# A hybrid retention and HGRN2 step on one core: level scores on column tiles, merged and moved short products, two-stream sums, and later starts of the first HGRN2 threads

## The chip, the cores and the metric

The kernel runs on one core of a Trainium2 chip, as one program. The metric is the device time of one execution in microseconds (us). Before the change it was 2616.91 us, the median of 3 runs (2615.58 to 2618.65). The engines of the core are named as in the profile: PE (TensorE, with PEld for its weight loads), DVE (VectorE), ACT (ScalarE), POOL (GpSimd) and SP (which issues most DMAs).

## The reference

One layer of a decoder for 272 prompt columns (16 meta tokens and 256 prompt tokens) and 8 sample columns, together 280, with a model width of 2048. A first half-step FFN (SwiGLU, width 5504) and a norm; a mixer; a norm; a second half-step FFN and a norm. The mixer projects `x @ w_in` to ten parts of 2048 and runs two recurrences:

```
def hgrn2_chunk(S, q, k, v, logf):
    b = jnp.cumsum(logf, axis=2)
    decay = exp(where(causal, b[i] - b[j], -inf))            # per feature d
    A = jnp.einsum('bhid,bhjd,bhijd->bhij', q, k, decay)
    o = einsum('bhij,bhjv->bhiv', A, v) + einsum('bhid,bhdv->bhiv', q * exp(b), S)
    S_new = exp(b_last) * S + einsum('bhjd,bhjv->bhdv', k * exp(b_last - b), v)
def retention_chunk(S, q, k, v):
    inner = einsum('bhid,bhjd->bhij', q, k) * D              # D: fixed decay per head
    o = einsum('bhij,bhjv->bhiv', inner, v) + einsum('bhid,bhdv->bhiv', q_dec, S)
    S_new = exp(lg * C) * S + einsum('bhjd,bhjv->bhdv', k_dec, v)
```

HGRN2 has 16 heads of 128, retention 8 heads of 256. The outputs are normed per head, gated, merged and projected by `w_out`. Prompt states and sample states are outputs too.

## The kernel before, in words

Features lie on the 128 partitions, tokens in the columns. A float32 weight block is streamed as 128x1024 raw values (`raw`, 512 KB a DMA, L184), cast on ACT to `whi` (L187), and its rest subtracted on DVE to `wlo` (L188); each such load serves 8 blocks of 128x128. `dense` (L203 to L219) does three matmuls a block: high by high, low by high, high by low, all of type float32r, with 264 or 280 columns. They are written as `Halves`: the columns lie in two halves and are read alternately, as two streams.

Phases in order: FFN 1 (L452), the projections with the mixer (L604 to L1075), the output projection, FFN 2, the last norm.

**The mixer's threads.** For each u from 0 to 7 there is a group of projections (`f, q_h, i_h, q_r, k_r, v_r`, each two column blocks of 128) and, one u later, the gates. After each of the 16 steps k of a projection, `dense` calls `pump` (L592), which counts down every open thread and, when a thread's count has run out, runs it to its next `yield n`; n is the number of pumps until it goes on. A thread is `mix_hg(u, ...)` (L713, two HGRN2 heads) or `mix_ret(u, ...)` (L945, one retention head). PE executes in the order in which this code writes its instructions (`manual_schedule`, L137): a thread's matmuls stand between two steps of a projection, and PE runs nothing past one that waits. The order on DVE, ACT and SP is set by a scheduler when the program is built; each engine then also works in that order. A thread is started by `start(gen, wait)` when its last projection is evacuated: `mix_hg` 3 pumps after `i_h`, but 30 for u = 1 (L642).

u = 0 is special: its first two groups of projections start before the first norm is finished. `Norm.first` and `Norm.second` (L365, L383) compute them on unnormed columns and correct the result on DVE (`corrected`, L388), while `normalise` (L402) writes the normed columns `xh` on ACT and `xl` on DVE (L407). For u = 0 the results `y` of `corrected` lie in row tiles, and for `i_h` ACT copies them to `v` (L639).

**mix_hg.** It makes Q, K and products on DVE and ACT (L716 to L744); then, for each of the two heads h, four transposes of `v` to a PSUM bank `pt` (L751: two of 128 columns, the 16 meta columns and the last 16), an ACT copy to `vth` (L752), an ACT copy of the last 16 to `vsm` (L753), a DMA of 8 of these rows to DRAM (L754) and the high and low parts `vm` of the first 16 (L755). `yield 1` stands after each head. Nine pumps later come sums over the features with a matrix of ones (`sums`, L227): `pd`, 512 columns, and per level `pl`. The causal score matrix `acc` is built in levels s = 1, 2, 4, 8, 16, 32, 64: in each, the second half of every pair of blocks of s tokens looks at the first half.

- s = 1 and 2: sums with ones (L782, L784), then DVE copies under a mask (L852).
- s = 4 and 8: one product of K (128 columns) with 192 columns for each head and half (L771).
- s = 16: four products of 128 key columns with 64 query columns each (L799), then one masked DVE copy (L852).
- s = 32: eight products of 32 by 32 on column tiles 0 and 64 of PE (`tile_position=(0, j)`, L794), then ACT copies.
- s = 64: four products of 64 by 64, all on the column tile at 0 (L789), then one ACT copy (L847).

Later steps: transposes of K (L868), states (L887, L889), the sample product `pq` on four column tiles (L901), an ACT copy `osh` of it (L905) and, 4 pumps later, the outputs (L912, L913, L709) and norms, with pauses of `8 + calm`.

**mix_ret.** Transposes of v and k (L965, L974), three score products in `psc` (L991; the third has 16 keys and 16 queries), the prompt state `psr` (L1008, seven float32r matmuls of 256 columns a half), the sample state `smr` scaled on ACT (L1025) and updated on DVE (L1028), the sample product `pqr` (L1039, two halves of 256 columns that DVE adds at L1044), then outputs (L1053) and the norm.

Plain float32 products appear in the records as two matmuls each, float32r products and transposes as one.

Of the kernel before, what the change touches and what calls it, by code (L numbers as in the profile page):

```python
# [14 lines left out]
ALU = mybir.AluOpType  # L15
# [3 lines left out]
P = 128  # L19
# [26 lines left out]
MASKED = 5  # L46

MASKS = {1: [0], 2: [1, MASKED], 4: [2], 8: [3, MASKED + 1], 16: [4]}
# [79 lines left out]
def trunk(ctx: ExitStack, tc: tile.TileContext, A, O):  # L128
# [98 lines left out]
    def sums(out, hilo, part=slice(None)):  # L227

        for i, x in enumerate(hilo):
            if isinstance(x, Halves):  # L230
                o, x = pairs(out), x[:]
            else:
                o, x = out, x[:, part]
            nc.tensor.matmul(o, ones_r, x, start=i == 0, stop=i == 1)
# [33 lines left out]
    class Norm:  # L268
# [114 lines left out]
        def second(self, block, outs, x0s):  # L383
            dense(block, KC, outs, xh, xl, [slice(x0, self.n + 2) for x0 in x0s])
            self.normalise()
            return self.corrected(outs, x0s)

        def corrected(self, outs, x0s):  # L388
            ys = []
            for i, (o, x0) in enumerate(zip(outs, x0s)):  # L390
                w = self.n - x0
                wgb = rp.tile([P, 2], F32, tag=f"wgb{i}", name="wgb")
                nc.scalar.copy(wgb, o[:, w : w + 2])
                y = self.row(("ls1", "ls2", "lnq", "rt")[i])[:, :w]
                nc.vector.scalar_tensor_tensor(
                    out=y, in0=self.mean[:, x0:], scalar=wgb[:, 0:1], in1=o[:, :w], op0=ALU.mult, op1=ALU.subtract)
# [134 lines left out]
    with tc.tile_pool(name="yp", bufs=1) as yp:  # L531
# [7 lines left out]
        with tc.tile_pool(name="mp", bufs=1) as mp:  # L539
# [37 lines left out]
            vsm = tmp("vsm", (P, 2, P))  # L577
# [26 lines left out]
            def project(groups):  # L604
                for grp in groups:

                    bank = mx_bank if grp[0] == (QKV_ORDER[2], 0) else acc_bank
                    outs = [bank(f"pj_{n}{c}") for n, c in grp]
                    x0s = [NMETA if n in LIVE else 0 for n, _ in grp]
                    if grp[0] == (QKV_ORDER[0], 0):  # L610
                        outs = norm1.first(block, outs, x0s)
                    elif grp[0] == (QKV_ORDER[2], 0):
                        outs = norm1.second(block, outs, x0s)
                    else:
                        dense(block, KC, outs, xh, xl, [slice(x0, T) for x0 in x0s], pump)
                    for j in range(0, len(grp), 2):
                        w = T - x0s[j]
                        evacuate(grp[j][0], grp[j][1], grp[j + 1][1], outs[j][:, :w], outs[j + 1][:, :w])

            def evacuate(n, c0, c1, o0, o1):  # L620
# [16 lines left out]
                elif n == "i_h":  # L637
                    v = tmp("v", (P, 2, T))
                    nc.scalar.copy(v[:, 0, :], o0)  # L639
                    nc.scalar.copy(v[:, 1, :], o1)  # L640

                    start(mix_hg(c0 // 2, st["f"], st["k"], st["q"], v), 30 if c0 == 2 else 3)  # L642
# [70 lines left out]
            def mix_hg(u, f, k, q, v):  # L713
# [31 lines left out]
                vt = tmp("vth", (P, 2, 2, P))  # L745
                vrow = []
                for h in range(2):

                    pt = mx_bank("pt")
                    for b, (t0, n) in enumerate(((NMETA, P), (NMETA + P, P), (0, NMETA), (T - NMETA, NMETA))):  # L750
                        nc.tensor.transpose(pt[:n, b * P : (b + 1) * P], v[:, h, t0 : t0 + n], ident)  # L751
                    nc.scalar.copy(vt[:, h], pt[:, : 2 * P].rearrange("p (b f) -> p b f", b=2))  # L752
# [6 lines left out]
                sums(pd.rearrange("p (i c) -> p i c", i=2), hilo, slice(0, 2))  # L759
                nc.vector.tensor_tensor(  # L760
                    out=acc.rearrange("p (b c) -> p b c", b=4), in0=pd.rearrange("p (b c) -> p b c", b=4),
                    in1=ident.unsqueeze(1).to_broadcast([P, 4, P]), op=ALU.mult)
                Tt = f
                for s in LEVELS:
# [18 lines left out]
                    elif s == 2:  # L783
                        sums(pl.rearrange("p (i c) -> p i c", i=2), hilo)  # L784
                    for h in range(2 if s > 8 else 0):
                        for b in range(2):
                            k0, q0, o = NMETA + b * P, b * P, (2 * h + b) * min(s, 64)
                            if s == 64:
                                nc.tensor.matmul(  # L789
                                    pl[0:s, o : o + s], K[:, h, k0 : k0 + s], Q[:, h, q0 + s : q0 + 2 * s],  # L790
                                    start=True, stop=True)
                            elif s == 32:
                                for j in (0, 64):
# [51 lines left out]
                    elif s >= 32:  # L845
# [4 lines left out]
                    else:  # L850
                        for j, mi in enumerate(MASKS[s]):
# [3 lines left out]
                                pl[:, j * SEQ : (j + 1) * SEQ].rearrange("p (n s) -> p n s", s=s))  # L855
# [72 lines left out]

                hilo = outputs(0)
# [15 lines left out]
            def mix_ret(u, q, k, v):  # L945
# [43 lines left out]
                for b, (col, l0, n, nk) in enumerate(SCORES):  # L989
                    for c in range(2):  # L990
                        nc.tensor.matmul(  # L991
                            psc[:nk, col : col + n], k[:, c, b * P : b * P + nk], q[:, c, l0 : l0 + n],
                            start=c == 0, stop=c == 1)
# [3 lines left out]
                mul(scr2[:NB2], psc[:NB2, c2:NSC], dt[:NB2, c2:])  # L997
                upper_upper_lower(sc2, scr2[:NB2])
# [3 lines left out]
                for c in range(2):  # L1002
                    pst = mx_bank("psr")
                    f = slice(c * P, (c + 1) * P)
                    pairs = [(ks[:, i, b, f], vs[:, j, b, :]) for b in range(2) for i, j in ((0, 0), (0, 1), (1, 0))]
                    pairs.append((ks2[:, c, :], vs2.rearrange("p c f -> p (c f)")))
                    for i, (kk, vv) in enumerate(pairs):
                        nc.tensor.matmul(pst[:, :256], kk, vv, start=i == 0, stop=i == 6)  # L1008
                    so = tmp("sro", (P, 256))
                    nc.scalar.copy(so, pst[:, :256])  # L1010
# [193 lines left out]
```

## Time and profile before

| what | value |
|---|---|
| median of 3 runs | 2616.91 us |
| the profiled execution | 2617.9 us |
| its span in the trace | 2616.1 us (1.8 us less) |
| mean granted TensorE clock | 0.998 |
| DVE busy | 1738.8 us (66%) |
| ACT busy | 1358.7 us (52%) |
| DMA | 536.26 MB, mean 205 GB/s |

The profile shows one execution. Its page gives busy time by engine, the span in 40 slices, the chain of work that ended last, and the costliest groups of instructions. The trace behind it answers finer questions: waits (who waited for whom), a timeline of single instructions in a window, and busy time and granted clock by window. Times in the timeline are in us from the span's start. A row of the timeline has the start, the time until its last instruction's end, engine, line, operation, what is written from what, shape, and how many instructions the row merges; in brackets the idle time before it and what ended that. Matmuls overlap: the distance between the starts of two rows tells what a matmul costs PE, not the time from its start to its end. Times before 770 us belong to FFN 1, from 740 to 1770 to the mixer, after that to the output projection and FFN 2.

### The profile page before, as it was taken

The page shows a single profiled execution, that of the slowest core. Times are in us where ns is not written, and L with a number is a line of the kernel's source. Part 1 is how long each engine was busy: PE and PEld are TensorE (multiplying, and loading weights), DVE is VectorE, ACT ScalarE, POOL GpSimd, SP SyncE. Part 2 cuts the span into 40 slices and gives each one's busy share as a digit, 9 for nine tenths or more (in the row PEclk, how much of TensorE's full clock was granted, in tenths as well). Part 3 has the DMA queues.
Part 4 walks back from the last instruction along what each step waited for, and adds up shares of the span by engine and source line. Part 5 has one row for each costly group of instructions (what it writes and reads, how often), then busy time and mean ns, then how long its engine had stood idle before and what let it go on. Part 6 is the DMA issues. An engine that isn't in the chain of part 4 may idle for free.

```text
span 2616.1 us, 54489 instructions
## 1 busy us (share of the span) xinstructions
PE 2593.6 (99%) x22576; PEld 2563.8 (98%) x22576; DVE 1738.8 (66%) x2961; ACT 1358.7 (52%) x2124; POOL 3.3 (0%) x38
## 2 busy tenths in 40 slices
PE   9999999999998999999999999999999999999999
PEld 9999999999998999999999999999999999999998
DVE  6445444565579788777878787876995555556555
ACT  5444444444465567656566656565564444444444
POOL 0000000000000000000000000000000000000000
PEclk9999999999999999999999999999999999999999
DMA  7555555565566786767676767666656666666664
GB/s 245 184 185 185 186 186 185 179 186 185 185 197 196 236 266 204 240 207 256 215 241 212 251 213 246 218 228 193 193 184 203 194 196 197 195 195 194 196 197 148
DMA packets 154584, 536.26 MB, mean 205 GB/s; under 512 B 17696, under 2 KB 25696, under 8 KB 154336
## 3 DMA queue, kind: packets, MB, share of 16 engines
q1 hardware_dynamic: 154048, 532.50, 63.5%
q8 instruction: 176, 2.88, 0.4%
q14 instruction: 72, 0.59, 0.1%
q10 hardware_dynamic: 288, 0.29, 0.0%
HBM read 502.12 MB, written 30.61 MB: 204 GB/s over the span
## 4 chain that ended last, share of the span: by engine, by line
PE 91%; DVE 5%; DMA 2%; ACT 1%; issue 1%; SPq 0%; DVEq 0%; ACTq 0%
PE up L217 35%; PE dn L217 18%; PE pj_k_r L217 3%; PE wo L217 3%; PE pj_q_h L217 3%; PE pj_v_r L217 3%; PE pj_g_r L217 3%; PE pj_f L217 3%; PE pj_q_r L217 3%; PE pj_g_h L217 3%; PE pj_a_r L217 3%; PE pj_a_h L217 3%; PE pj_i_h L217 3%; DVE wlo L188 2%; DMA smr<-in_sr 1%
## 5 line engine op out<-in xcount | busy, mean ns | idle before, releaser
L188 DVE TENSOR_TENSOR wlo<-raw,whi 128x1024 fp32r<-128x1024 f32 (+1 forms) x869 | 1061.8, 1223 | 718.5 <-ACT whi L187 711.0
L187 ACT CAST whi<-raw 128x1024 fp32r<-128x1024 f32 (+1 forms) x870 | 905.1, 1042 | 912.6 <-PE up L217 409.5
L217 PE MATMUL up<-xh,wlo 128*128 128x280 f32 (+1 forms) x2624 | 725.9, 280 | 0.4 <-DVE wlo L188 0.2
L217 PE MATMUL up<-xh,whi 128*128 128x280 f32 (+1 forms) x2624 | 725.6, 280 | 0.4 <-ACT whi L187 0.4
L217 PE MATMUL up<-xl,whi 128*128 128x280 f32 (+1 forms) x2624 | 725.4, 279 | 0.0
L217 PEld LDWEIGHTS up<-xh,wlo 128*128 128x128 f32 x2624 | 492.6, 189 | 1.2 <-DVE wlo L188 1.2
L217 PEld LDWEIGHTS up<-xh,whi 128*128 128x128 f32 x2624 | 492.6, 189 | 0.6 <-ACT whi L187 0.6
L217 PEld LDWEIGHTS up<-xl,whi 128*128 128x128 f32 x2624 | 492.6, 189 | 0.0
L217 PE MATMUL dn<-hh,whi 128*128 128x280 f32 (+1 forms) x1376 | 384.7, 280 | 0.0
L217 PE MATMUL dn<-hh,wlo 128*128 128x280 f32 (+1 forms) x1376 | 384.3, 279 | 0.0
L217 PE MATMUL dn<-hl,whi 128*128 128x280 f32 (+1 forms) x1376 | 384.3, 279 | 0.0
L217 PEld LDWEIGHTS dn<-hh,whi 128*128 128x128 f32 x1376 | 260.1, 189 | 0.1
L217 PEld LDWEIGHTS dn<-hl,whi 128*128 128x128 f32 x1376 | 260.1, 189 | 0.1
L217 PEld LDWEIGHTS dn<-hh,wlo 128*128 128x128 f32 x1376 | 260.1, 189 | 0.0
L217 PE MATMUL pj_g_r<-xh,whi 128*128 128x264 f32 x256 | 76.9, 300 | 0.0
L217 PE MATMUL pj_g_h<-xh,whi 128*128 128x264 f32 x256 | 73.5, 287 | 0.1
L217 PE MATMUL pj_v_r<-xh,whi 128*128 128x280 f32 x256 | 73.6, 288 | 0.0
L217 PE MATMUL pj_k_r<-xh,whi 128*128 128x280 f32 x256 | 73.5, 287 | 0.0
L217 PE MATMUL pj_g_h<-xh,wlo 128*128 128x264 f32 x256 | 71.1, 278 | 2.0 <-DVE wlo L188 2.0
L217 PE MATMUL pj_k_r<-xh,wlo 128*128 128x280 f32 x256 | 72.8, 284 | 0.1
L217 PE MATMUL pj_k_r<-xl,whi 128*128 128x280 f32 x256 | 72.7, 284 | 0.0
L217 PE MATMUL pj_v_r<-xl,whi 128*128 128x280 f32 x256 | 72.3, 283 | 0.0
(402 smaller groups left out, 5285.2 us busy)
## 6 DMA issues: line engine op xcount, KB each, us to landing
raw<-in_w_up SPq DMA_DIRECT2D x343, 512.0 KB, 4.2
raw<-in_w_in SPq DMA_DIRECT2D x320, 512.0 KB, 3.7
raw<-in_w_dn SPq DMA_DIRECT2D x172, 512.0 KB, 3.5
smr<-in_sr SPq DMA_DIRECT2D x32, 512.0 KB, 4.3
out_srs<-smr SPq DMA_DIRECT2D x32, 512.0 KB, 5.5
raw<-in_w_out SPq DMA_DIRECT2D x32, 512.0 KB, 3.4
smh<-in_sg SPq DMA_DIRECT2D x16, 512.0 KB, 4.8
vbr<-vrd SPq DMA_DIRECT2D x16, 512.0 KB, 4.3
```

The costliest lines, as they stand in the source:

```text
L187: nc.scalar.copy(hi[:, j:jn, :], raw[:, j:jn, :])
L188: nc.vector.tensor_tensor(out=lo[:, j0:j1, :], in0=raw[:, j0:j1, :], in1=hi[:, j0:j1, :].bitcast(F32), op=ALU.subtract)
L217: nc.tensor.matmul(o, w, t, start=start, stop=stop)
```

## The change

1. `sums` reads a pair of products as two streams: columns of the two products alternate, in `pd` and in `pl` of level 2. DVE reads the results with a step of two, and `pd` is multiplied by the identity in two DVE instructions for one.
2. `Norm.second` can write its result to a given place: for u = 0, `i_h` goes straight to `v`, without the ACT copies.
3. The thread of u = 0 starts 20 pumps after `i_h` (3 before), that of u = 1 46 pumps after (30 before). For u = 0 the pauses in the outputs are 8 (10 before).
4. In `mix_hg` the short transposes go: DVE copies the first and the last 16 columns of both heads to a tile `ends` (two copies), and one transpose of `ends` (64 columns) follows the two long transposes of head 1 and the ACT copy `vth` of head 1, in the same bank `pt`. `vsm`, the row DMAs and `vm` of both heads come after it.
5. Level 16: sixteen products of 16 by 16, on the column tiles 0, 32, 64 and 96; ACT copies in place of the masked DVE copy (and one mask less). Level 64: its two halves b on the column tiles 0 and 64; two ACT copies for one.
6. In `mix_ret` the third score product moves from `psc` to the bank of `pqr`, just ahead of the sample product, and so do the steps that follow it (`scr2`, `sc2`); the two halves of `pqr` are accumulated in PSUM, without DVE's add.
7. The prompt state `psr` reads `vs` as two streams; ACT copies the result with a step of two.

The diff, cut to its core:

```diff
@@ sums
+            elif len(x.shape) == 3 and x[:, part].shape[1] == 2:
+                o, x = pairs(out), x[:, part].rearrange("p a b -> p b a")
@@ Norm.corrected
-                nc.vector.tensor_scalar(out=y, in0=y, scalar1=-1.0, scalar2=wgb[:, 1:2], op0=ALU.mult, op1=ALU.add)
-                ys.append(y)
+                to = into[i] if i < len(into) else y
+                nc.vector.tensor_scalar(out=to, in0=y, scalar1=-1.0, scalar2=wgb[:, 1:2], op0=ALU.mult, op1=ALU.add)
+                ys.append(to)
@@ project, evacuate
-                        outs = norm1.second(block, outs, x0s)
+                        v = st["i_h"] = tmp("v", (P, 2, T))
+                        outs = norm1.second(block, outs, x0s, (v[:, 0, :], v[:, 1, :]))
-                    start(mix_hg(c0 // 2, st["f"], st["k"], st["q"], v), 30 if c0 == 2 else 3)
+                    start(mix_hg(c0 // 2, st["f"], st["k"], st["q"], v), {0: 20, 2: 46}.get(c0, 3))
@@ mix_hg
                 vt = tmp("vth", (P, 2, 2, P))
+                ends = tmp("ends", (P, 2, 2, NMETA))
+                nc.vector.tensor_copy(ends[:, :, 0, :], v[:, :, :NMETA])
+                nc.vector.tensor_copy(ends[:, :, 1, :], v[:, :, T - NMETA :])
                 for h in range(2):
                     pt = mx_bank("pt")
-                    for b, (t0, n) in enumerate(((NMETA, P), (NMETA + P, P), (0, NMETA), (T - NMETA, NMETA))):
-                        nc.tensor.transpose(pt[:n, b * P : (b + 1) * P], v[:, h, t0 : t0 + n], ident)
+                    for b in range(2):
+                        nc.tensor.transpose(pt[:, b * P : (b + 1) * P], v[:, h, NMETA + b * P : NMETA + (b + 1) * P], ident)
                     nc.scalar.copy(vt[:, h], pt[:, : 2 * P].rearrange("p (b f) -> p b f", b=2))
-                    nc.scalar.copy(vsm[:NMETA, h, :], pt[:NMETA, 3 * P :])
-                    vrow.append(rows_out(vsm[8:16, h, :], P, f"vh{h}"))
-                    upper_lower_upper(vm[:, h, :], pt[:NMETA, 2 * P : 3 * P])
+                    if h:
+                        x = pt[:64, 2 * P : 3 * P]
+                        nc.tensor.transpose(x, ends.rearrange("p c a t -> p (c a t)"), ident)
+                        nc.scalar.copy(vsm[:64], x)
+                        for c in range(2):
+                            vrow.append(rows_out(vsm[32 * c + 24 : 32 * c + 32, :], P, f"vh{c}"))
+                            upper_lower_upper(vm[:, c, :], x[32 * c : 32 * c + NMETA])
                     yield 1
@@ levels 16, 32, 64
                             if s == 64:
+                                j = 64 * b
                                 nc.tensor.matmul(
-                                    pl[0:s, o : o + s], K[:, h, k0 : k0 + s], Q[:, h, q0 + s : q0 + 2 * s],
-                                    start=True, stop=True)
-                            elif s == 32:
-                                for j in (0, 64):
+                                    pl[j : j + s, h * s : (h + 1) * s], K[:, h, k0 : k0 + s], Q[:, h, q0 + s : q0 + 2 * s],
+                                    start=True, stop=True, tile_position=(0, j))
+                            else:
+                                for j in range(0, P, 2 * s):
                                     nc.tensor.matmul(
                                         pl[j : j + s, o : o + s], K[:, h, k0 + j : k0 + j + s],
                                         Q[:, h, q0 + j + s : q0 + j + 2 * s], start=True, stop=True, tile_position=(0, j))
-                            else:
-                                o = (2 * h + b) * 64
-                                nc.tensor.matmul(
-                                    pl[:, o : o + 64], K[:, h, k0 : k0 + P],
-                                    Q[:, h, q0 : q0 + P].rearrange("p (n t s) -> p n t s", t=2, s=s)[:, :, 1, :],
-                                    start=True, stop=True)
+                calm = calm if u else 0
@@ mix_ret
-                for b, (col, l0, n, nk) in enumerate(SCORES):
+                for b in range(2):
+                    scores(psc[:, SCORES[b][0] :], b)
-                mul(scr2[:NB2], psc[:NB2, c2:NSC], dt[:NB2, c2:])
-                upper_upper_lower(sc2, scr2[:NB2])
-                        nc.tensor.matmul(pst[:, :256], kk, vv, start=i == 0, stop=i == 6)
+                        nc.tensor.matmul(pairs(pst[:, :256]), kk, vv.rearrange("p c f -> p f c"), start=i == 0, stop=i == 6)
-                    nc.scalar.copy(so, pst[:, :256])
+                    nc.scalar.copy(so.rearrange("p (c f) -> p c f", c=2), apart(pst[:, :256]))
                 pq = mx_bank("pqr")
+                scores(pq[:, 256:], 2)
-                                pq[32 * j : 32 * j + 32, 256 * e : 256 * e + 256], qdr[:, c, 32 * b : 32 * b + 32],
-                                sms[2 * e + c][:, j, :], start=c == 0, stop=c == 1, tile_position=(0, 32 * j))
+                                pq[32 * j : 32 * j + 32, :256], qdr[:, c, 32 * b : 32 * b + 32],
+                                sms[2 * e + c][:, j, :], start=e + c == 0, stop=e + c == 2, tile_position=(0, 32 * j))
+                mul(scr2[:NB2], pq[:NB2, 256 : 256 + NMETA], dt[:NB2, c2:])
+                upper_upper_lower(sc2, scr2[:NB2])
-                add(os, os, pq[:, 256:])
```

`scores(out, b)` is a new local function with the two accumulating products of one block b of `SCORES`, as L992 has them.

More of the change, by code (lines that the diff above doesn't have):

```diff
@@ L45 @@
 LEVELS = (1, 2, 4, 8, 16, 32, 64)
-MASKED = 5
-MASKS = {1: [0], 2: [1, MASKED], 4: [2], 8: [3, MASKED + 1], 16: [4]}
+MASKED = 4
+MASKS = {1: [0], 2: [1, MASKED], 4: [2], 8: [3, MASKED + 1]}
 W_LEVEL = 6
@@ L381, in first, with second, corrected @@
             return ys
-        def second(self, block, outs, x0s):
+        def second(self, block, outs, x0s, into=()):
             dense(block, KC, outs, xh, xl, [slice(x0, self.n + 2) for x0 in x0s])
             self.normalise()
-            return self.corrected(outs, x0s)
-        def corrected(self, outs, x0s):
+            return self.corrected(outs, x0s, into)
+        def corrected(self, outs, x0s, into=()):
             ys = []
@@ L758, in mix_hg @@
                 pd = mx_bank("pd")
[L759 to L762, printed above, removed]
+                sums(pd, hilo, slice(0, 2))
+                for h in range(2):
+                    nc.vector.tensor_tensor(
+                        out=acc[:, 2 * P * h : 2 * P * (h + 1)].rearrange("p (b c) -> p b c", b=2),
+                        in0=pd.rearrange("p (b c h) -> p h b c", b=2, h=2)[:, h],
+                        in1=ident.unsqueeze(1).to_broadcast([P, 2, P]), op=ALU.mult)
                 Tt = f
```

35 lines of the change are left out of this document (22 added, 13 removed).

## The prediction

> **What bounds the kernel now.** I read the page first, for the engine that fills the span, then the waits of PE, then windows and the timeline where PE stands still.
>
> ```profile
> span 2616.1 us, 54489 instructions
> ...
> PE 2593.6 (99%) x22576; PEld 2563.8 (98%) x22576; DVE 1738.8 (66%) x2961; ACT 1358.7 (52%) x2124; POOL 3.3 (0%) x38
> ```
>
> PE is busy for 99% of the span. So an edit is worth what it takes from PE's own stream, or from a place where PE holds still. Work on DVE (66%) and ACT (52%) costs nothing unless PE waits for it. The two holds of PE that the change touches:
>
> ```profile
> PE pt L751 <- ACT v L639: 7.4, 1, 7.4
> PE po L709 <- ACT osh L905: 2.1, 1, 2.1
> ```
>
> The first is at the first head's transposes. Rows of PE in order of time (start, length):
>
> ```profile
> 790.37 0.28 PE L217 MATMUL pj_k_r<-xh,whi 128*128 128x280 f32 x1
> ...
> 800.48 1.12 PE L751 MATMUL pt<-ident,v 128*128 128x128 f32 x4 [7.43 <-ACT v L639]
> ```
>
> ACT is only the last link: `v` is copied from results of `corrected`, which stand late in the queue of DVE. The window of its end (length, busy time of PE, PEld, DVE, ACT and POOL, granted clock, DMA share, GB/s):
>
> ```profile
> 800.00:805.00 5.00, 4.52 (x25) 4.22 (x26) 5.00 (x13) 3.65 (x11) 0.00 (x0) 0.60 0.01 2
> ```
>
> DVE works all the time. From 800.48 on PE works at a mean granted clock of about 0.60 for 4.5 us: some 1.8 us of work are lost on top. The hold costs 7.4 + 1.8 = 9.2 us.
>
> **The change part by part.** All sums are against the profiled execution: 2617.9 us, 1.8 above its span and 1.0 above the median of 2616.91 us.
>
> *The first hold.* The thread of u = 0 now starts 17 pumps later, and `v` is written by DVE itself: the 9.2 us go (**-9.2**). But the new transpose of `ends` behind head 1 waits for two DVE copies, and in the order of instructions in the built program these stand far back. DVE around this time:
>
> ```profile
> 798.04 0.92 DVE L395 SCALAR_TENSOR_TENSOR ls<-lnc,wgb,pj_i_h 128x280 f32<-128x280 f32 x2
> ...
> 802.17 0.43 DVE L648 SCALAR_TENSOR_TENSOR q_r<-lnq,cos 128x264 f32<-128x264 f32 x1
> ...
> 803.92 1.23 DVE L188 TENSOR_TENSOR wlo<-raw,whi 128x1024 fp32r<-128x1024 f32 x1
> 805.06 0.43 DVE L650 TENSOR_TENSOR q_r<-q_r,rot 128x264 f32<-128x264 f32 x1
> 805.41 0.68 DVE L237 TENSOR_TENSOR Q<-q,f 128x512 f32<-128x512 f32 x1
> ...
> 806.66 0.75 DVE L237 TENSOR_TENSOR pr<-q,k 128x256 f32<-128x256 f32 x2
> ...
> 809.25 1.09 DVE L225 TENSOR_TENSOR prodvbh<-pr,prodsmh 128x256 fp32r<-128x256 f32 x3
> ```
>
> DVE is full, so I keep its anchor: the corrections run from 798.04 to 802.17. In the new order follow one rotary operation (0.35 from 805.06 to 805.41), three `wlo` (1.14 each, from 803.92 to 805.06), eleven rotary operations (3.85), two `wlo` (2.28), Q, K and the small copies (1.25, from 805.41 to 806.66), three `pr` (1.1) and three low parts (1.1), and then the `ends` copies (0.26, an estimate by the small copies that are inside the 1.25). That is 802.17 + 0.35 + 3.42 + 3.85 + 2.28 + 1.25 + 1.1 + 1.1 + 0.26 = 815.8. PE arrives at 790.37 + 21 steps of six matmuls (0.714 each) = 805.4, with 0.9 us of small waits for `wlo` on the way and 0.44 for the four long transposes: 806.7. It **waits 9.1 us**, with `wlo` of the next steps behind nothing but PE itself. I add 0.6 for the small waits that before did not have and the half clock again at 1.7 (0.9 if it is gone sooner, 3.4 for twice the stretch): **+11.4**. What goes at the first head comes back at the second.
>
> *The `ends` transpose in the other groups.* It writes the bank that ACT's copy `vth` of head 1 reads, so PE stands until that copy is done. In a later u, PE and then ACT:
>
> ```profile
> 1149.86 0.60 PE L751 MATMUL pt<-ident,v 128*128 128x128 f32 x4
> ```
>
> ```profile
> 1150.35 1.05 ACT L187 CAST whi<-raw 128x1024 fp32r<-128x1024 f32 x1
> 1151.30 0.37 ACT L752 COPY vth<-pt 128x256 f32<-128x256 f32 x1
> ```
>
> Before, PE went straight on: four transposes take 0.60, a single matmul is 0.28 from start to end in the rows of dense, so a further transpose costs (0.60 - 0.28) / 3 = 0.11. ACT's copy came 1.4 us after the transposes, behind a cast of the next weights, and nobody minded. In the new order ACT has the cast between the two `vth` for u = 2 to 7, and the cast starts about when the transposes do, since a matmul just ahead of them frees its buffer. Cast 0.95, copy 0.37, 0.14 to get in and out: the third transpose can go 1.46 after the first and wanted to at 0.22. That is 1.24 held and some 0.1 for the restart, times six: **+8.0**. For u = 1 the two copies stand back to back, 0.7: **+0.7**. The bounds for a head are 0.63 (the cast is long done) and 1.9 (the cast starts late): 4.4 to 13.3 for all seven. I take the built order as it stands.
>
> *Fewer transposes.* For each u eight transposes become five, 3 x 0.11 x 8: **-2.6**.
>
> *Levels 16 and 64.* Level 16 before, with dense rows after it:
>
> ```profile
> 1179.34 0.28 PE L217 MATMUL pj_v_r<-xh,wlo 128*128 128x280 f32 x1
> ...
> 1180.47 0.28 PE L217 MATMUL pj_v_r<-xl,whi 128*128 128x280 f32 x1
> ...
> 1184.52 0.28 PE L217 MATMUL pj_v_r<-xh,wlo 128*128 128x280 f32 x1
> ```
>
> A dense matmul is (1184.52 - 1180.47) / 34 = 0.119 for 280 columns, 0.426 ns a column. Level 16 costs 1.13 - 0.24 = 0.89. Level 32, already on two column tiles, and the four tiles of the sample product:
>
> ```profile
> 1185.88 0.28 PE L217 MATMUL pj_a_r<-xh,wlo 128*128 128x264 f32 x1
> 1186.08 0.45 PE L794 MATMUL pl<-Q,K 128*32 128x32 f32 x16
> 1186.46 0.38 PE L217 MATMUL pj_g_r<-xh,whi 128*128 128x264 f32 x1
> 1186.67 0.28 PE L217 MATMUL pj_g_r<-xl,whi 128*128 128x264 f32 x1
> ```
>
> ```profile
> 1225.76 1.08 PE L901 MATMUL pq<-smh,qdh 128*32 128x128 f32 x32
> ```
>
> Level 32 costs 0.79 - 0.225 = 0.565 with the way into the tiles and out, for eight rounds of two records (0.38). New level 16 is eight rounds of four records. If a round of four takes a round of two: 0.565, so -0.33, **-2.6** for eight u. If each record needs what one takes now (0.38 / 16 = 0.024), 16 more cost 0.38: 0.95, +0.5 in all. `pq` shows 32 records of 128 columns side by side in 1.08, 0.034 for a record four times as wide as level 32's; so four do run at once, and I take the first. The Trainium skill speaks against it: "TensorEngine Tiling (Array Packing)", Instruction Overhead, says that every matmul has some 60 cycles of overhead and that no tiling factor should be taken from a dimension that is small already, as here (16 columns). By that page this part would be near the second end, and the total 3 us above mine; whether the overhead of four tiles is shared no row of this shape shows. Level 64 on one tile:
>
> ```profile
> 1195.12 0.68 PE L789 MATMUL pl<-Q,K 128*64 128x64 f32 x8
> ```
>
> 0.68 against level 32's 0.45, both with the same entry: on two tiles I expect 0.45, -0.23, **-1.8** (0 if the two do not overlap). Both are read by more ACT copies than before (five a u), in 48% free time of ACT.
>
> *The third score product.*
>
> ```profile
> 1193.59 0.73 PE L991 MATMUL psc<-q_r,k_r 128*128 128x144 f32 x7
> ...
> 1194.46 0.28 PE L217 MATMUL pj_g_r<-xl,whi 128*128 128x264 f32 x1
> ```
>
> Without the last product 0.87 falls to some 0.48: -0.39. In `pqr`, whose entry into column tiles is a pause already, it costs 0.11 to 0.2: net -0.25, **-2.0**. Its readers `scr2` and `sc2` have seven pumps before the outputs need them. DVE's add goes, off the path.
>
> *Two streams.*
>
> ```profile
> 1196.51 0.99 PE L1008 MATMUL psr<-vs,ks 128*128 128x256 f32 x7
> ```
>
> ```profile
> 1157.05 0.40 PE L234 MATMUL pd<-prodsmh,ones_r 128*128 128x512 f32 x1
> 1157.28 0.39 PE L234 MATMUL pd<-prodvbh,ones_r 128*128 128x512 f32 x1
> ```
>
> `psr`: (0.99 - 0.28) / 6 = 0.118 a matmul of 256 columns; at the dense pace 0.109; 112 of them, -1.0. The sums: 0.23 for 512 columns against 0.218, 32 of them, -0.4. Together **-1.5**. The dense streams lie in halves of a column block; streams 512 or 1024 bytes apart are in no row, so the other end is the same loss, +1.5.
>
> *The hold at `osh`.* For u = 1 ACT's copy stood behind the scaling of `smr`, which waited for a DMA. In the new order it stands ahead of that. The start of u = 1 moves, so another may take its place: of 2.1 I take **-1.0** (0 to -2.1).
>
> **Sum:** -9.2 + 11.4 + 8.0 + 0.7 - 2.6 - 2.6 - 1.8 - 2.0 - 1.5 - 1.0 = -0.6. The profiled execution would take 2617.3 us, the median some 2616.
>
> **The rivals.**
>
> *The first hold does go* (faster). If PE does not stand at `ends` for u = 0, because DVE gets to it before PE (it would need 9 us less queue, or PE 13 steps later), the 11.4 is not paid: 2616 - 11 = 2605 us. For it: the start was far too early by just this hold, and 20 pumps are 14 us. Against it: the order of DVE, full from 798 to 812.
>
> *The tiles do not run side by side* (slower). If short products on different column tiles follow each other, each record at a pair's time of level 32 (0.048), level 16 takes 32 x 0.048 + 0.185 = 1.72 against 0.89, +6.6 in place of -2.6, and level 64 gains nothing, +1.8: 2616 + 9.2 + 1.8 = 2627 us. It decides from 22 ns a record: above that, 32 records cost more than the 0.71 that old level 16 leaves beside the entry. For it: no row has four tiles with so few columns. Against it: `pq`.
>
> *The heads do not wait*: if the scheduler's cast is over in time, 0.63 a head, 2612 us; this lies in the forecast's own range.
>
> **How the numbers follow.** A difference under 0.2% (5.2 us) is about what a measurement of this kernel cannot tell from none: same is 2611.7 to 2622.1. The forecast's own range: heads -4.3 to +4.6, level 16 up to +3.1, level 64 up to +1.8, streams up to +3.0, clock -0.8 to +1.7; not all at once, 2611 to 2623. Chances: forecast 0.64 (0.50 of it within the bound, 0.06 below, 0.08 above), first hold gone 0.23, tiles one by one 0.13. So faster 0.29, same 0.50, slower 0.21. The range reaches to the faster rival, 2605 to 2624, and leaves out the slower one and the lower half of the faster.
>
> **What would show it.** Right: the idle before `pt<-ident,ends` is 9 us once, near 807 to 816, with DVE as releaser and a dip of the granted clock behind it, and 1.2 us six times with ACT's `vth` as releaser; the row of level 16 is about 0.5 long with 32 records, that of level 64 0.45 with 8; `psr` x7 is 0.93; `psc` has no x7 row. Wrong: no long idle time of PE near 807 (2605), a level 16 row above 0.9 (slower), `psr` above 0.99 (streams), or an idle of 7 us elsewhere, which I would have missed.

## The result and the profile after

The changed kernel takes 2623.14 us (median of 17 runs, 2615.84 to 2628.92), the kernel before, run beside it, 2619.01 us (17 runs, 2615.58 to 2622.80). The ratio is 1.0018, with a 95% interval of 1.0011 to 1.0024: it is slower by a little under 0.2%, 4 to 5 us, where the prediction had it 0.6 to 1 us faster. The profiled execution took 2620.37 us, its span is 2618.3 us; it is one of the faster ones. The page's first lines and the waits of PE in the changed kernel (who waited, for whom, us in total, times, longest):

```profile
span 2618.3 us, 54877 instructions
...
PE 2584.3 (99%) x22744; PEld 2554.2 (98%) x22744; DVE 1736.0 (66%) x2969; ACT 1363.9 (52%) x2152; POOL 3.3 (0%) x38
```

```profile
PE pt L764 <- DVE ends L754: 8.7, 1, 8.7
PE pt L764 <- ACT vth L761: 7.0, 7, 1.1
PE pl L805 <- DVE Q L239: 3.4, 1, 3.4
PE pj_g_h L217 <- DVE wlo L188: 2.6, 4, 0.8
PE pt L991 <- DVE acch L790: 1.5, 1, 1.5
PE psr L1026 <- DVE ks L997: 1.4, 3, 1.0
```

PE is busy for 9.3 us less than before (2593.6), and the span is 2.2 us longer: the saved work is there, and more than that went into waiting. The waits at `osh` (2.1) and `v` (7.4) of before are gone. Both waits at `ends` stand where the prediction put them, at 8.7 and 7.0 us. The third and fifth row are new, and the sixth has grown from 0.4; all lie mainly in the first two groups. The fourth row, at the gates, was there before too:

```profile
PE pj_g_h L217 <- DVE wlo L188: 2.0, 3, 0.8
```

The wait at `ends` for u = 0, and the window behind it (length, busy PE, PEld, DVE, ACT, POOL, granted clock, DMA share, GB/s):

```profile
815.00:820.00 5.00, 4.56 (x25) 4.59 (x26) 4.81 (x20) 2.56 (x8) 0.00 (x0) 0.63 0.04 9
```

A later head, PE and then ACT:

```profile
1147.79 0.38 PE L760 MATMUL pt<-ident,v 128*128 128x128 f32 x2
1149.25 0.30 PE L764 MATMUL pt<-ident,ends 128*64 128x128 f32 x1 [1.07 <-ACT vth L761]
```

```profile
1147.88 1.04 ACT L187 CAST whi<-raw 128x1024 fp32r<-128x1024 f32 x1 [0.19 <-PE pj_q_r L217]
1148.83 0.36 ACT L761 COPY vth<-pt 128x256 f32<-128x256 f32 x1
```

The cast starts 0.09 us after the first transpose, the copy follows it, and the third transpose starts 1.46 us after the first: what the prediction had worked out from the built order, to the hundredth.

The short products (start, length; what they cost is the distance to the dense rows around them):

```profile
1178.36 0.28 PE L217 MATMUL pj_v_r<-xh,wlo 128*128 128x280 f32 x1
1178.58 0.39 PE L810 MATMUL pl<-Q,K 128*16 128x16 f32 x32
1178.89 0.39 PE L217 MATMUL pj_v_r<-xh,whi 128*128 128x280 f32 x1
1179.11 0.28 PE L217 MATMUL pj_v_r<-xl,whi 128*128 128x280 f32 x1
...
1191.25 1.52 PE L1009 MATMUL psc<-q_r,k_r 128*128 128x256 f32 x8
...
1193.37 0.45 PE L805 MATMUL pl<-Q,K 128*64 128x64 f32 x8
...
1194.54 0.94 PE L1026 MATMUL psr<-vs,ks 128*128 128x256 f32 x7
```

```profile
1156.14 0.38 PE L236 MATMUL pd<-prodsmh,ones_r 128*128 128x512 f32 x1
1156.36 0.38 PE L236 MATMUL pd<-prodvbh,ones_r 128*128 128x512 f32 x1
```

Level 16 costs 1179.11 - 1178.36 - 0.24 = 0.51 where it cost 0.89. Its 32 records take 0.31 us together, 10 ns apiece. The Trainium skill's rule against it ("TensorEngine Tiling (Array Packing)", Instruction Overhead: some 60 cycles for every matmul, no tiling of a dimension that is small already) is not borne out for this shape on four column tiles: the measured row decides, and a round of four records did not cost more than a round of two. Level 64 is 0.45 long, and `psr` 0.94 for 0.99, both as forecast. Streams 512 bytes apart (`psr`) and 1024 bytes apart (`pd`, 0.22 us from row to row where it was 0.23) go at the dense pace.

So every product is about as short as predicted and both waits about as long, and still the sum failed. The start of the same dense matmul in several executions shows where. Differences to the first profiled execution of the kernel before, in us, from the timelines; the two further executions of the changed kernel and the one of before are among the experiments below:

| matmul, and its time before | changed, 1st | changed, 2nd | changed, 3rd | before, 2nd |
|---|---|---|---|---|
| `pj_k_r`, 806.66 (u = 0) | -10.12 | -9.91 | -10.04 | +2.66 |
| `pj_v_r`, 819.26 | +0.04 | +0.59 | +0.65 | +2.67 |
| `pj_q_r`, 1020.38 (u = 2) | +1.50 | -1.49 | +1.52 | +1.65 |
| `pj_g_h`, 1785.47 (end of the mixer; `wo` starts at 1812) | +2.21 | +5.22 | +5.62 | +1.13 |

The first hold is removed and comes back at `ends` (first two rows). At u = 2 the kernels are even. From there to the end of the mixer the changed kernel loses 0.7, 6.7 and 4.1 us. By the prediction's own terms it should gain 1.2 there: 6 x 1.31 of shorter products less 5 x 1.34 of waits for `vth`.

### The profile page after: what moved, and what is told of

The parts are those of the page before. It is cut to its first block, busy times and chain, and to the rows that moved or that the text cites. A ratio compares the mean times of both kernels' runs of the same rounds, so it can differ in the third digit from the quotient of the medians.

```text
span 2618.3 us, 54877 instructions
## 1 busy us (share of the span) xinstructions
PE 2584.3 (99%) x22744; PEld 2554.2 (98%) x22744; DVE 1736.0 (66%) x2969; ACT 1363.9 (52%) x2152; POOL 3.3 (0%) x38
## 4 chain that ended last, share of the span: by engine, by line
PE 89%; DVE 6%; DMA 3%; ACT 2%; issue 1%; SPq 0%; DVEq 0%; ACTq 0%
PE up L217 35%; PE dn L217 18%; PE wo L217 3%; PE pj_f L217 3%; PE pj_v_r L217 3%; PE pj_q_h L217 3%; PE pj_q_r L217 3%; PE pj_k_r L217 3%; PE pj_i_h L217 3%; PE pj_g_r L217 3%; PE pj_a_r L217 3%; PE pj_g_h L217 2%; PE pj_a_h L217 2%; DVE wlo L188 2%; DMA smr<-in_sr 1%
## 5 line engine op out<-in xcount | busy, mean ns | idle before, releaser
L217 PE MATMUL pj_v_r<-xh,wlo 128*128 128x280 f32 x256 | 73.0, 285 | 0.0
```

Source lines behind the costliest of these rows:

```text
L217: nc.tensor.matmul(o, w, t, start=start, stop=stop)
```

## The experiments

Theory A, formed from the first trace: the loss is in waits, at `ends` and where the later first threads meet DVE. Rival B: PE only arrives earlier at something else that is late. Rival C: the starts cost nothing elsewhere. All times are medians; a ratio is to the kernel before, run on the same chips, with its 95% interval. The changed kernel has 1.0018 (1.0011 to 1.0024).

**1. The transpose of `ends` first.**

```diff
                     pt = mx_bank("pt")
+                    if h:
+                        x = pt[:64, 2 * P : 3 * P]
+                        nc.tensor.transpose(x, ends.rearrange("p c a t -> p (c a t)"), ident)
                     for b in range(2):
...
                     if h:
-                        x = pt[:64, 2 * P : 3 * P]
-                        nc.tensor.transpose(x, ends.rearrange("p c a t -> p (c a t)"), ident)
                         nc.scalar.copy(vsm[:64], x)
```

> The changed kernel with one edit: for head 1 the transpose of `ends` stands ahead of the two long ones, so it no longer follows ACT's reading of its bank. Theory A (the loss is in waits that were added at `ends` and in waits that the later first threads met): the seven waits for `vth`, 7.0 us, go and nothing takes their place, -7 us against the changed kernel, about 2616. Rival B (these waits only delay PE to where it would wait anyhow, the next weights): less than 2 us gained, 2621 to 2623. In both the wait of 8.7 us for DVE's `ends` stays.

Measured: 2617.66 us, 0.9995 (0.9986 to 1.0004), 0.23% or 6 us below the changed kernel. In its profile the waits for `vth` are gone, but this row has grown from 2.6:

```profile
PE pj_g_h L217 <- DVE wlo L188: 5.3, 8, 0.8
```

Theory A holds for the time. The row looks like a sign of rival B, but it is none by itself: two further executions of the unedited changed kernel have 5.0 and 4.0 there (experiments 13 and 14).

**2. The copies to `ends` early.** They are written where `v` is complete, and `ends` is handed to the thread.

```diff
+                    ends = tmp("ends", (P, 2, 2, NMETA))
+                    nc.vector.tensor_copy(ends[:, :, 0, :], v[:, :, :NMETA])
+                    nc.vector.tensor_copy(ends[:, :, 1, :], v[:, :, T - NMETA :])
-                    start(mix_hg(c0 // 2, st["f"], st["k"], st["q"], v), {0: 20, 2: 46}.get(c0, 3))
+                    start(mix_hg(c0 // 2, st["f"], st["k"], st["q"], v, ends), {0: 20, 2: 46}.get(c0, 3))
```

> The changed kernel with one edit: the two DVE copies to `ends` are written right after v, before the thread starts, so they stand ahead of the rotary operations, Q, K and the products in DVE's order. Theory A: at u = 0 the wait of 8.7 us falls to about the 1.1 us that the other heads wait for ACT, and the half clock behind it (about 1.7 us) goes with it: -9 us, about 2614. Rival B (DVE is what is late there, and PE meets it a few steps on, at the next low weights): most of the 8.7 us comes back as waits for `wlo` between 807 and 830, gain under 3 us.

Measured: 2618.97 us, 1.0001 (0.9992 to 1.0010), 4 us below the changed kernel, half of what theory A gave and more than rival B's 3. The hold at `ends` for u = 0 is 0.7 us. In exchange PE waits for DVE at 815 (`pd`), 831 (`psr`) and 859 (`pl`), which are half of the first and all of the second and fourth of these rows:

```profile
PE psr L1026 <- DVE ks L997: 3.4, 4, 1.7
PE pl L805 <- DVE Q L239: 2.3, 1, 2.3
PE pt L991 <- DVE acch L790: 1.5, 1, 1.5
PE pd L236 <- DVE prodvbh L225: 1.1, 1, 1.1
```

DVE is what is late there: it is busy for 99% of the time from 790 to 845, and for 85% from 845 to 865. A hold that is removed there comes back in smaller ones, and in this execution the clock stays up (1.00 granted in every window from 790 to 865, against 0.63 to 0.69 between 810 and 820 in the changed kernel).

**3. The starts of before** (3 and 30 pumps, and the pauses of u = 0 as before) in the changed kernel.

```diff
-                    start(mix_hg(c0 // 2, st["f"], st["k"], st["q"], v), {0: 20, 2: 46}.get(c0, 3))
+                    start(mix_hg(c0 // 2, st["f"], st["k"], st["q"], v), 30 if c0 == 2 else 3)
...
-                calm = calm if u else 0
```

> The changed kernel with the starts of the first two threads and the pauses of u = 0 as before (3 and 30 pumps). Theory A: the waits of PE for Q at level 64 of u = 0 (3.4 us, and about 1.7 of half clock behind it), for the masked copies (1.5) and for ks (1.4) go; the waits at osh and smr of before (3.5 in all) come back; the first hold is split into one for v (about 7) and one for `ends`, 9 to 15 us in all against 8.7 + 1.7: between 2617 and 2623. Rival C (the starts cost nothing elsewhere, all of the loss is at `ends`): no wait but those at the first thread changes, and the time is that of the changed kernel plus what the first hold grows, 2623 to 2628.

Measured: 2631.16 us, 1.0052 (1.0040 to 1.0065), above both ranges. PE holds twice: 7.0 us before the first transposes of `v`, 7.3 for `ends`, and the clock is low all along (0.50 granted from 800 to 810, 0.54 from 810 to 815). Q and the masked copies are gone from the waits and `osh` is back at 2.4, as theory A said; that is worth less than the second hold and the low clock cost.

**4. The starts alone,** in the kernel before (20 and 46 pumps, pauses of 8 for u = 0).

> The kernel before with one part of the change alone: starts of 20 and 46 pumps and the pauses of u = 0 at 8. Theory A: the hold for v (7.4 us and 1.8 of half clock) goes, since v is there 12 us later, but the later threads meet waits that cost some 4 to 5 net (Q behind the sample state, masked copies, ks, less osh and smr): about 2614. Rival C (the starts cost nothing elsewhere): all 9 us are gained, about 2610. Rival D (the hold for v is only moved, since DVE is behind): no gain, 2619.

Measured: 2616.69 us, 0.9988 (0.9979 to 0.9997), -3 us, between theory A and rival D. The hold of 7.4 is gone, and in its profile PE waits between 815 and 865 for `prodsmh`, `prodvbh`, ks, K and Q, 0.7 to 2.5 each, 6.1 us together. Rival C is out: the starts do cost something elsewhere.

**5. The short products alone.** Starts and transposes as before, everything else of the change kept.

> The changed kernel with the starts, the pauses of u = 0 and the eight transposes of v a pair of heads as before: left are the levels 16 and 64, the moved third score product and the two-stream sums. By the rows of the two profiles these save 8 x (0.38 + 0.23 + 0.33) + 1.4 = 9 us of PE. Theory A (PE's time is bound by its own stream there): -9 us against the kernel before, about 2610, with the first hold (7.4 us) unchanged. Rival B (PE only arrives earlier at the next weights): waits of `pj` matmuls for `wlo` grow by as much as is saved, and the gain is under 4 us, 2615 to 2619.

Measured: 2620.05 us, 1.0007 (0.9998 to 1.0016), 10 us above theory A and 1 above rival B's range: no gain from some 8 to 9 us of shorter products. Theory A falls here. Where the time went:

```profile
PE pj_g_h L217 <- DVE wlo L188: 6.7, 10, 0.8
```

against 2.0 (3 times) in the kernel before; one or two such waits stand at the ends of six groups. The chain behind one, ACT in this kernel from 1489 to 1503, with a row of DVE and one of PE:

```profile
1489.16 0.38 ACT L914 COPY osh<-pq 128x256 f32<-128x256 f32 x1
1495.43 1.06 ACT L1035 ACTIVATE smr<-smr 128x1024 f32<-128x1024 f32 x1 [5.89 <-DMA smr<-in_sr]
1496.39 0.37 ACT L666 ACTIVATE gs<-pj_g_r 128x264 f32<-128x264 f32 x1
1496.66 1.03 ACT L187 CAST whi<-raw 128x1024 fp32r<-128x1024 f32 x1
1497.60 0.39 ACT L669 ACTIVATE gs<-pj_a_r 128x264 f32<-128x264 f32 x1
1497.73 1.23 DVE L188 TENSOR_TENSOR wlo<-raw,whi 128x1024 fp32r<-128x1024 f32 x1 [0.50 <-PE pj_a_h L217]
...
1499.01 0.38 PE L217 MATMUL pj_g_h<-xh,wlo 128*128 128x264 f32 x1 [0.77 <-DVE wlo L188]
...
1501.75 1.03 ACT L187 CAST whi<-raw 128x1024 fp32r<-128x1024 f32 x1
```

and the same place in the kernel before:

```profile
1493.78 1.06 ACT L1025 ACTIVATE smr<-smr 128x1024 f32<-128x1024 f32 x1 [3.79 <-DMA smr<-in_sr]
1494.75 0.37 ACT L660 ACTIVATE gs<-pj_g_r 128x264 f32<-128x264 f32 x1
1495.02 1.03 ACT L187 CAST whi<-raw 128x1024 fp32r<-128x1024 f32 x1
1496.09 1.23 DVE L188 TENSOR_TENSOR wlo<-raw,whi 128x1024 fp32r<-128x1024 f32 x1 [0.51 <-ACT whi L187]
```

ACT stands at the scaling of the sample state until its DMA lands. Behind it in ACT's order are the gates and the cast of the next weights; DVE's `wlo` follows the cast, PE's matmul `wlo`. A PE that is earlier finds ACT still waiting, and waits itself. The same dense matmuls in the two profiles give the price: the ends of the groups (from `pj_g_h` at 1228, 1361, 1491 and 1621 in time of before to the next `pj_f`, some 15 us each) take 1.9, 2.1, 2.5 and 0.7 us longer in this kernel, 7.2 together. In windows around 1490 the DMA engines are busy 0.8 to 1.0 of the time in both kernels, and the pair of loads, issued at 1488.02 here and 1489.11 before, let ACT go on 7.4 us later here and 4.7 before. Why the same two loads take longer is open; they did, with some overlap, in every kernel with the short products (5.1 to 7.8 us from 1219 on, and 4.4 to 6.0 in the two without). This is theory E; its opposite, rival F in the texts below, is that the transfers themselves are late, wherever the scaling is done. The prediction had nothing of either.

**6. The eight transposes of before,** all else as changed.

> The changed kernel with part 4 alone undone: four transposes of v for each head as before, no `ends`. Theory A: both waits at `ends` (8.7 and 7.0 us) go, three more transposes for each u cost 2.6, and DVE's backlog around 815 to 865 takes back what it took in the late-start kernel (some 4 us): -9 us against the changed kernel, about 2614 or lower, down to 2608 if the gains of the short products and of the late starts add up. Rival B: no more than the 5 us that the other order of `ends` gave, 2618.

Measured: 2611.82 us, 0.9975 (0.9966 to 0.9984), 11 us below the changed kernel, inside theory A's range. Part 4 of the change alone turns a gain of 6.5 us into a loss of 4.7.

**7. Both edits of `ends`** (1 and 2).

> The changed kernel with both edits of `ends` at once: its copies right after v, and its transpose ahead of the long ones of head 1. Theory A: the two gains add, -5.5 and -4.2 us, about 2613 to 2614, and no wait at `pt` is left. Rival B (what is saved at one comes back at the other or at the next low weights): 2616 to 2618.

Measured: 2610.52 us, 0.9967 (0.9955 to 0.9980), 13 us below the changed kernel, more than the two alone (6 + 4) and than either theory gave. Its only wait at `pt` of `mix_hg` is 0.6 us.

**8. Shorter pauses between the levels of u = 0** (`calm` is 0 for it from the start). The wait at level 64 that this was to remove, DVE and then PE in the changed kernel:

```profile
861.45 2.46 DVE L1046 SCALAR_TENSOR_TENSOR smr<-vbr,k_r,smr 128x256 f32<-128x256 f32 x6 [3.12 <-DMA vbr<-vrd]
...
866.43 0.42 DVE L239 TENSOR_TENSOR Q<-Q,T 128x256 f32<-128x256 f32 x1
```

```profile
867.00 0.70 PE L805 MATMUL pl<-Q,K 128*64 128x64 f32 x8 [3.42 <-DVE Q L239]
```

> The changed kernel with the pauses of u = 0 between its levels at 6 and 8 pumps in place of 8 and 10, so that level 32's products on K and Q stand ahead of the update of the sample state in DVE's order. Theory A (PE's wait of 3.4 us at level 64 of u = 0, and the half clock behind it, comes from DVE standing at that update for a DMA): both go, -5 us, about 2618; the spread of the run times narrows. Rival C (DVE is just behind at that place, whatever stands ahead): the wait stays in size or moves to an earlier level, 2621 to 2624.

Measured: 2626.60 us, 1.0035 (1.0022 to 1.0047), slower. At that place PE no longer waits for Q, and a few steps on this wait took its place:

```profile
PE ptk L884 <- DVE K L239: 4.0, 1, 4.0
```

Neither range has this time. In kind it is the case of rival C as this text has it (DVE is behind, whatever stands ahead), though the wait moved to a later step: DVE works 99% of 840 to 860 and 89% of 860 to 865, and the K that PE waits for comes behind the update of the sample state again.

**9 to 12. The sample state scaled on POOL.** One line in four kernels; the arithmetic stays the same. 9 is the kernel before, 10 the short products alone, 11 the changed kernel, 12 the changed kernel with both edits of `ends`.

```diff
-                        nc.scalar.mul(sm, sm, GAMMA[u])
+                        nc.gpsimd.tensor_scalar(out=sm, in0=sm, scalar1=GAMMA[u], scalar2=None, op0=ALU.mult)
```

> The kernel before with one edit: the scaling of the sample state `smr` (128x1024, 32 times) is done on POOL, which is idle, in place of ACT. Theory E (in every group ACT stands at this scaling for its DMA, 4 to 6 us, with the cast of the next weights behind it, and PE meets that as waits for `wlo` at `pj_g_h`): the kernel before has only 2.0 us of such waits, so -1 to -3 us, about 2616. Rival F (the transfers of weights and states themselves are what is late): no change. If POOL slows DVE, both lose: 2620 or more.

> The kernel with the short products alone (starts and transposes as before), and the scaling of `smr` on POOL. With ACT's scaling it was 1.8 us slower than the kernel before although PE's short products are some 9 us shorter. Theory E: with ACT free of that DMA the waits at `pj_g_h` (6.7 us) go and the savings stay: 7 to 9 us below the kernel before with the same edit, about 2608. Rival F: within 2 us of the kernel before with the same edit.

> The changed kernel with the scaling of `smr` on POOL. Theory E: in the groups from u = 2 on its waits for `wlo` (2.6 us) and part of what surrounds them go, -3 to -6 us against the changed kernel, 2617 to 2620; the waits at `ends` (8.7 and 7.0 us) stay. Rival F: 2622 to 2624.

> The changed kernel with both edits of `ends` (copies right after v, transpose ahead of the long ones) and the scaling of `smr` on POOL. Theory E: 4 to 7 us below the kernel with the two edits alone (2610.5), about 2605. Rival F: 2609 to 2612.

| kernel | with ACT's scaling | with POOL's scaling |
|---|---|---|
| before | 1 | 2608.06 us, 0.9956 (0.9944 to 0.9969) |
| short products alone | 1.0007 (0.9998 to 1.0016) | 2605.38 us, 0.9945 (0.9933 to 0.9958) |
| changed | 1.0018 (1.0011 to 1.0024) | 2614.05 us, 0.9980 (0.9971 to 0.9989) |
| changed, both edits of `ends` | 0.9967 (0.9955 to 0.9980) | 2603.86 us, 0.9938 (0.9925 to 0.9952) |

No kernel with POOL's scaling has a wait at `pj_g_h` left. In the kernel before the edit is worth 12 us, far over the 1 to 3 that I expected from the listed waits; by the same dense matmuls 8.3 us of it arise between 825 and 1112, in the first groups, where `osh` (2.1) and the waits inside `pqr` go too. The short products now gain 2.7 us (some 2 either way, from five runs each) where they gained nothing: the sign is theory E's, the size is not (7 to 9), and rival F's bound was 2. In 11 the edit gives 10 us, where theory E gave 3 to 6, and in 12 some 8 (both by the ratios), where it gave 4 to 7; rival F is out in 9, 11 and 12. Over the four groups from 1118 to 1643 in time of before, where the first threads play no part, the spans are:

| kernel | ACT's scaling | POOL's scaling |
|---|---|---|
| before | 524.5 | 522.1 |
| short products alone | 527.6 | 519.2 |
| changed | 527.9 | 523.5 |
| changed, both edits of `ends` | 524.2 | 519.0 |

Each number is from one execution, and two executions more of the changed kernel have 530.8 and 529.7. On POOL the short products save 2.9 us here. PE's rows in this stretch give 4.6 (levels 2.4, score product 1.6, streams 0.6), and the rest goes to `pqr`, which is 1.7 longer: 0.3 of it is the product that moved there, the rest a wait for DVE's update of its operand. That update follows POOL, which takes 2.9 us for a scaling where ACT takes 1.06, but it also waits for a DMA (`vbr`, 2.3 and 2.6 us in the two groups where `pqr` is long), so that POOL is the reason is not shown. With ACT's scaling the same stretch is 3.1 longer than before. At the ends of the four groups, where the short products lost 7.2 us with ACT's scaling, they lose 0.0 with POOL's (10 against 9). There theory E is shown, with one thing open: the edit takes 32 scalings of 1.06 us off ACT as well as the wait in front of them, and no run separates the two; the idle time in the row above is 5.89.

POOL's scaling is not free for DVE: between `before` and 9 DVE's busy time grows from 1738.8 to 1754.2 us with the same 2961 instructions. What 9 gains is in spite of that.

The difference between 11 and 12 (10 us) comes again from the two edits of `ends`.

**13 to 15. Further executions** of the changed kernel (two) and of the kernel before.

> The changed kernel as it is, one more look. Theory E: up to u = 1 it stands within 1 us of the first look (the hold of 8.7 us and the waits for ACT are fixed by the order on the engines), and what differs comes at the ends of the groups from u = 2 on, where ACT waits for the sample state. Theory A2: it differs by 2 us or more at the pause of level 64 of u = 0, where DVE waits for a DMA, and the half clock behind it.

> As the look before it: theory E says that the difference to the first look comes from the ends of the groups from u = 2 on, theory A2 from the pause at level 64 of u = 0.

> The kernel before as it is, one more look. Both theories: up to u = 1 it stands within 1 us of its first look. Theory E: a difference, if there is one, comes at the ends of the groups from u = 2 on, and is smaller than that between looks at the changed kernel.

Measured, one run each: 2623.43, 2623.80 and 2619.01 us. Their places in the table of the first section: up to 1020 the changed kernel stands at -1.5 to +1.5 (the wait for Q is 3.4, 1.1 and 1.9 in the three), so the place of theory A2, the pause at level 64 of u = 0, varies by 3 us, and theory E's "within 1 us up to u = 1" is wrong, for the kernel before too (+2.7 at 807, half of it from FFN 1); from there on it loses 0.7, 6.7 and 4.1, and before loses nothing. Most of what separates the median from the first profile is at the ends of the groups, as theory E has it. The waits at `pj_g_h` in the three:

```profile
PE pj_g_h L217 <- DVE wlo L188: 5.0, 8, 0.8
```

in the second, 4.0 in the third, 2.6 in the first.

## Why the prediction was wrong

- **The sum, in two halves.** By the prediction's terms part 4 costs 11.4 + 8.0 + 0.7 - 2.6 = 17.5 us and all the rest gains 18.1. By experiment 6 part 4 costs 11 and the rest gains 6.5. Both came out smaller than forecast; the gains shrank far more, and that turned the sign. That the total is still within 6 us of the forecast is luck: two errors cancel.
- **The first hold: right in place, too high in worth.** -9.2 and +11.4 were forecast, the table shows -10.1 and +10.2. "What goes at the first head comes back at the second" is what the trace shows; the wait is 8.7 for 9.1. But the terms count a hold that goes as gained in full. Experiment 2 removes the second hold and gains 4 us, experiment 4 removes the first and gains 3: DVE, late there, takes the rest back.
- **The other heads: right.** 8.7 forecast, 7.0 us of waits and 7 restarts measured; experiment 1 gives 6 us for them.
- **The short products: right in size on PE, wrong in what they are worth.** Level 16 -0.38 for -0.33 a group, level 64 -0.23 for -0.23, `psr` -0.05 for 7, the third score product -0.3 with its place in `pqr` (-0.39 and +0.07) for -0.25. The step that failed is that "the sum" counts these terms (-2.6, -1.8, -2.0 and -1.5, together -7.9 us) as gained in full, because PE is busy for 99% of the span and work on DVE (66%) and ACT (52%) was taken to cost nothing. The prediction never asked what PE meets next when it is earlier at the end of a group. Experiment 5 shows that the gain is nothing (+1.8 us, -0.5 to +4.2). Its profile loses 7.2 us at four group ends, and 9 to 12 show that these go when the sample state's scaling leaves ACT. Over the whole kernel that edit brings back 4.5 of the some 10 us between forecast and result; the rest meets other waits, at `pqr` among them, and is open.
- **The cover that was not named.** The prediction wrote that work on ACT "costs nothing unless PE waits for it". ACT's share was 52%, but it stood idle in front of a DMA with the next weights' cast behind that in its order. Before's own waits for `smr` (3.79 us in the row above) were in the trace, and PE's 2.0 us at `pj_g_h` were their visible end. The prediction had read this very stand of ACT at `osh`, and not asked where else it falls.
- **The late starts.** The prediction took them as moving one hold; they also moved the threads of u = 0 and u = 1 into a stretch where DVE is full. That gave waits at Q (3.4), the masked copies (1.5) and ks (1.0 more), and took away `osh` (2.1) and `pqr` (1.4). At 1020 all this is even, within 1.5 us.
- **The rivals.** Neither came: the first hold did not go, and the tiles do run side by side. What took place was a third case, waits that take the place of removed work, which the prediction listed only as "an idle of 7 us elsewhere".
- **Not settled:** why the two loads of the sample state land later with the short products, what part of POOL's 12 us in the kernel before is the cast and what part the gates, and where the short products lose the rest of their gain.

## What to carry to other kernels

An engine that is busy for 99% of the span can still be paced by another one: before counting shorter work as gained, look at what the next wait of that engine would be if it came a microsecond earlier, and at the longest idle time of every engine that feeds it. An instruction that waits for a DMA in the queue that also prepares the next operands can delay these by what is left of the wait; here an idle engine was the better place for it, even at 2.7 times the duration. In this kernel a transpose into a bank that another engine still reads waited for that reader and for what was queued ahead of it: put it ahead of the products whose copy it would wait for.

## What the hardware showed that was not expected

32 records of 16 columns on four column tiles took 0.31 us, 10 ns apiece, where 16 of 32 columns on two tiles take 0.38. Two streams 512 bytes apart are read at (0.94 - 0.28) / 6 = 0.110 us for 256 columns, the pace of the dense streams (0.109). Of the low clock after a hold of 8.7 us the executions differ: 0.63 granted between 815 and 820 in the first, 0.51 in the third. POOL's scalings lengthen DVE's instructions that run beside them: in experiment 9 the 39 `wlo` that overlap one take 1.34 us each, the others 1.22.
